# First weights in two half transfers, rounded by the vector engine alone, and the sink row's transfer on another queue

## The chip, the cores and the metric

The kernel runs on one core of one Trainium2 chip. The metric is the time of one execution on the device in microseconds (us); lower is better. A core has five engines that work at the same time, each through a queue of instructions of its own, in order: TensorE (PE in the profile, with its weight loads as PEld), VectorE (DVE), ScalarE (ACT), GpSimd (POOL) and SyncE (SP), which here does nothing but issue transfers between memory and the on-chip buffers. ACT and POOL issue transfers too. An instruction that has to wait for a semaphore holds up everything behind it in its engine's queue.

## The reference

A two-layer encoder on 256 tokens of 1024 values, in float32. Layer 0 mixes tokens with a gated short convolution, layer 1 with windowed attention (16 heads, 4 key and value heads, a window of 128 tokens, a relative bias and one "sink" logit per head). After each mixer stands the same kind of expert layer, called PEER. Cut to what matters:

```python
for i in range(2):
    x = x + (conv_mixer if i == 0 else attention)(rmsnorm(x, g[i]))
    x = x + peer(rmsnorm(x, ffn_g[i]), ...)
return rmsnorm(x, final_norm_g)

# conv mixer:  gate_b, gate_c, h = split(x @ w_in, 3);  (gate_b * conv3(gate_c * h)) @ w_out
# attention:   softmax over [scores + bias, sink] (the sink column is dropped afterwards)
# peer:        per token and head, top 16 of 16384 experts by two sub-key products, then
#              sum over the picked e of  softmax(gate)[e] * gelu(x . u[e]) * v[e]
```

## The kernel before, in words

**Split numbers.** TensorE multiplies in a rounded float32 format. To keep precision, every weight tile (128 x 1024) and every activation is held as two parts: the rounded value `hi` and the remainder `lo = raw - hi`. A product is three products: hi by hi, lo by hi, hi by lo. So each weight tile goes through three steps: SP's queue issues its transfer into `raw` (four buffers), an engine rounds it into `hi` (three buffers), and DVE subtracts to get `lo` (two buffers). The function `split_tile` does this. In the usual form ACT rounds (line 197) and DVE makes the remainder of the whole tile (line 198). A buffer comes free only when its last reader is done, so a late `lo` on DVE also delays the transfers that reuse `raw`.

**The beginning.** The convolution mixer starts with `turned_x` (its `else` branch, lines 490 to 512). PE first multiplies zeros (`keep_warm`), transposes the input `x` into `xn`, and multiplies zeros twice more. ACT scales the eight transposed pieces k = 0 to 7 into `xn[:, k, :T]` (line 502), except k = 1, which DVE does (line 499). Then the first weight tile is prepared by a form of `split_tile` of its own: one transfer of 512 KB, and three casts, of columns 0 to 255 and 256 to 511 on DVE and 512 to 1023 on POOL (line 190); DVE then makes the remainder in two halves (line 194) and the remainders of `xn` (line 508). The next two weight tiles come in the usual form, but rounded by ACT in halves. `first_three` (line 273) writes out the order in which PE takes these three tiles: for the first one k = 0 to 5 of `hi`, k = 0 to 3 of `lo`, k = 6 and 7 of `hi`, then k = 4 to 7 of `lo`; after it the `hi` of the other two, and the rest. One k is 128 columns of the weight tile, so k = 0 to 3 is its first half.

**The expert layer.** `peer` runs over 128 rows of u (128 experts each) in its first half of the work, and over 128 rows of v in its second (the loop over j in steps of 2 at line 1353). The gates with which rows are weighted are put into tables in device memory by indirect transfers that add single values, issued by POOL (line 666). Part of them, the "far additions", go in 22 steps of four transfers; `far_pump` issues one step at a time: four during the last 16 rows of the first half of the work, then one for every two rows of v from j = 0 on. Later rows load their gates back from these tables (line 1277).

While the second half of layer 0's `peer` runs, `meanwhile` prepares the attention: from j = 64 on, every fourth j calls `prepare_attention(part)` with part 0, 1, 2 and so on. Part 0 takes the memory that the first 64 rows of layer 0 no longer need and loads the sink row into it, broadcast to 128 partitions (line 735); parts 0 to 7 load the bias (line 737); part 8 (j = 96) negates the sink row on DVE (line 1390).

**What sets the order.** The program is written as one stream. The framework draws up each engine's queue before the run: instructions go in the order of the code, but one whose inputs its plan holds to be ready may go ahead of earlier ones when its engine is free in that plan. Where the code says `with tc.issue_after(ins)`, what is traced inside on the engine of `ins` stays behind `ins`; instructions on other engines are not bound by it. `meanwhile` is called inside such a block, behind ACT's copy (line 1347) of the rows in hand. `bg.behind` is the last instruction of this kind on DVE. Semaphores for data are set by the framework.

Of the kernel before, what the change touches and what calls it, by code (L numbers as in the profile page):

```python
# [17 lines left out]
P = 128  # L18
T = 256
D = 1024  # L20
NT = T // P
KC = D // P
HEADS = 16
# [53 lines left out]
def trunk_kernel(  # L77
# [20 lines left out]
    nc = tc.nc  # L98
    V, S, G, PE = nc.vector, nc.scalar, nc.gpsimd, nc.tensor
# [11 lines left out]
    def matmul(*a, **k):  # L111
        newest[:] = [PE.matmul(*a, **k).ins]  # L112
        return newest[0]

    def transpose(*a):
        newest[:] = [PE.transpose(*a).ins]  # L116
        return newest[0]

    def in_turn():

        return tc.issue_after(newest[0])
# [53 lines left out]

    roomy = []

    def split_tile(src, spare=False, pieces=1, engines=()):
        raw = strm.tile([P, D], F32, tag="raw", name="raw", bufs=4)
        hi = strm.tile([P, D], F32R, tag="hi", name="hi", bufs=3)  # L180
        if roomy:
            roomy[0] = not roomy[0]
            spare = roomy[0]
        lo = strm.tile([P, D], F32R, tag="oh2" if spare else "lo", name="lo", bufs=2)
        nc.sync.dma_start(raw, src)
        halves = slice(0, D // 2), slice(D // 2, D)
        if engines:
            at = 0
            for n, engine in engines:
                engine.tensor_copy(hi[:, at : at + n], raw[:, at : at + n])  # L190
                at += n
            for c in halves:
                with tc.issue_after(bg.behind):
                    bg.behind = V.tensor_tensor(lo[:, c], raw[:, c], hi[:, c].bitcast(F32), ALU.subtract).ins
            return hi, lo
        for c in halves if pieces > 1 else (slice(0, D),):
            bg.rounded = S.copy(hi[:, c], raw[:, c]).ins  # L197
        bg.behind = V.tensor_tensor(lo, raw, hi.bitcast(F32), ALU.subtract).ins  # L198
        return hi, lo
# [22 lines left out]
    def take(n=2):  # L222

        prefetch(n)
        return ahead.popleft()

    def prefetch(n, *how):
        while order and len(ahead) < n:
            with ExitStack() as held:
                for ins in evicted:  # L230
                    held.enter_context(tc.issue_after(ins))
                ahead.append(split_tile(order.popleft(), *how))
# [40 lines left out]
    def first_three(b, act):  # L273

        w = [[a.rearrange("p (k c) -> p k c", k=KC) for a in take(3 - i)] for i in range(3)]
        turns = [(0, 0, k, 0) for k in range(6)] + [(0, 1, k, 0) for k in range(4)]
        turns += [(0, 0, k, 0) for k in (6, 7)] + [(0, 1, k, 0) for k in range(4, KC)]
        later = (1, 0, 0), (2, 0, 0), (0, 0, 1), (1, 0, 1), (2, 0, 1), (1, 1, 0), (2, 1, 0)
        turns += [(i, low, k, n) for i, low, n in later for k in range(KC)]
        for at, (i, low, k, n) in enumerate(turns):  # L280
            others = [turn[0] == i for turn in turns]
            with in_turn():
                matmul(
                    b[i], w[i][low][:, k], act[:, k, T * n : T * n + T],
                    start=not any(others[:at]), stop=not any(others[at + 1 :]),
                )
            if at == 5 * KC - 1:
                prefetch(1, True)
            if at == 8 * KC - 1:
                prefetch(2)  # L290
        chain[:] = newest
# [70 lines left out]
    def add_to_x(acc, t, h):  # L362
        c = slice(512 * h, 512 * h + 512)
        return V.tensor_tensor(xs[:, t, c], acc[t][h], xs[:, t, c], ALU.add).ins
# [26 lines left out]
    def turned_x(n, xn, last=None, opens=None):  # L391
# [30 lines left out]
        def turn_by_halves(i):  # L422

            t, h = parts[i]
            if i == 0:
                banks.extend(bank("g", "ptr").rearrange("p (k c) -> p k c", k=2) for _ in range(2))
            if h:
                own = [bank("acc", "ptr").rearrange("p (k c) -> p k c", k=4) for _ in range(1 + 2 * t)]
                banks.append([own[min(j, 2 * t)][:, j] for j in range(4)])
            for j in range(4):  # L430
                k = 4 * h + j
                to = banks[-1][j] if h else banks[j // 2][:, j % 2, P * t : P * t + P]
                transpose(to, xs[:, t, P * k : P * k + P], ident)
# [7 lines left out]
        def high_of(h, t=0):  # L441
            for j in range(4):
                k, c, b = parted(h, t, j)
                evicted[:] = [S.activation(xn[:, k, c], b, AF.Copy, scale=gain[:, n, k : k + 1]).ins]

        def low_of(h, t=0, j0=0, j1=4):
            for j in range(j0, j1):
                k, c, b = parted(h, t, j)
                V.scalar_tensor_tensor(
                    xn[:, k, T + c.start : T + c.stop], b, gain[:, n, k : k + 1], xn[:, k, c].bitcast(F32),  # L450
                    op0=ALU.mult, op1=ALU.subtract,
                )

        if last:
            acc, one = last
            parts = [(t, h) for h in range(2) for t in range(NT)]
            for i in range(2):
                one(*parts[i])
                add_to_x(acc, *parts[i])
            prefetch(1, True)  # L460
            turn_by_halves(0)
            one(*parts[2])
            added = add_to_x(acc, *parts[2])
            turn_by_halves(1)
            high_of(0)
            with tc.issue_after(added):
                low_of(0, 0, 0, 3)

            def third():
                with in_turn():  # L470
                    turn_by_halves(2)
                high_of(1, 0)

            one(*parts[3], between=third)
            added = add_to_x(acc, *parts[3])
            with tc.issue_after(added):
                low_of(0, 0, 3, 4)
                low_of(1, 0)
            product = opened(opens, ahead.popleft(), xn)
            next(product)  # L480
            with in_turn():
                turn_by_halves(3)
            high_of(1, 1)
            low_of(1, 1)
            for _ in product:
                pass
            prefetch(1)
            evicted[:] = [bg.rounded]
        else:
            own = [bank("acc" if i > 1 else "g", "ptr").rearrange("p (k c) -> p k c", k=2) for i in range(6)]  # L490
            banks.extend([own[k][:, 0] if k < 4 else own[2 + k // 2][:, k % 2] for k in range(KC)])
            for t in range(NT):
                for k in range(KC):
                    turned = transpose(banks[k][:, P * t : P * t + P], xs[:, t, P * k : P * k + P], ident)
            with tc.issue_after(turned):
                keep_warm(WARM[1])
            for k in range(KC):
                if k == 1:
                    bg.behind = V.tensor_scalar(xn[:, k, :T], banks[k], gain[:, n, k : k + 1], None, op0=ALU.mult).ins
                else:  # L500
                    evicted[:] = [
                        S.activation(xn[:, k, :T], banks[k], AF.Copy, scale=gain[:, n, k : k + 1]).ins  # L502
                    ]
            with tc.issue_after(bg.behind):
                prefetch(1, False, 1, ((T, V), (T, V), (D // 2, G)))
            for k in range(KC):
                with tc.issue_after(bg.behind):
                    bg.behind = V.scalar_tensor_tensor(
                        xn[:, k, T:], banks[k], gain[:, n, k : k + 1], xn[:, k, :T].bitcast(F32),
                        op0=ALU.mult, op1=ALU.subtract,  # L510
                    ).ins
            prefetch(3, False, 2)
# [218 lines left out]
    def load_bias(sc, part):  # L731

        if part == 0:
            sc.held = sc(HEADS, 384), sc(HEADS)
            nc.scalar.dma_start(sc.held[1], bass.AP(tensor=sink.tensor, offset=sink.offset, ap=[[0, P], [1, HEADS]]))
        h = 2 * part
        nc.scalar.dma_start(
            sc.held[0][:, h : h + 2],
            bass.AP(
                tensor=bias_dram.tensor,  # L740
                offset=bias_dram.offset + h * 511,
                ap=[[1, P], [511, 2], [1, 384]],
            ),
        )
# [635 lines left out]
    sc = Scratch("HA", "mix0")  # L1380
# [169 lines left out]
```

## Time and profile before

| | |
|---|---|
| median of 3 runs | 1732.43 us (1732.32 to 1732.75) |
| the profiled execution: time, span | 1732.49 us, 1730.7 us |
| PE busy | 1722.7 us |
| DVE, ACT, POOL busy | 1384.9, 944.3, 970.3 us |
| transfers | 390.93 MB, mean 226 GB/s |

The span is the profiled part of the execution, from the first to the last instruction that the profiler records. A row of the timeline has the start, the length, the engine, the line of the code, the operation, the tile written and the tile read, their shapes, and how many instructions were merged into the row; in brackets stands how long the engine was idle before it and what ended that. "ACTq" or "POOLq" is the issue of a transfer by that engine. `pv`, `ph` and `pconv` are accumulators of PE; `raw`, `hi` and `lo` are the weight tiles; `mix` is scratch memory, which the sink row and the bias share. A row of the stretches has the window, its length, the busy time of PE, PEld, DVE, ACT and POOL, each with its count, the granted clock, the share of the transfer engines and GB/s. A row of the groups has the busy time and the mean in ns behind the bar, then the idle time before the group and what ended it. A row of transfer issues ends with the median time from issue to landing.

### The profile page before, as it was taken

Reading aid. Unit: us, or ns where it says so; the run is one execution under the profiler, and the core shown is the slowest. Engines: PE = TensorE matmul, PEld = TensorE weight load, DVE = VectorE, ACT = ScalarE, POOL = GpSimd, SP = SyncE. Lnnn points to the kernel's source line nnn. Section 1 sums busy time; section 2 is a strip of 40 time slices with the busy share of each in tenths; the row PEclk is TensorE's granted clock in tenths of the full one; section 3 lists DMA queues with packets and bytes.
Section 4 is the critical chain, followed back from the end, with each engine's and each line's share of the span. In section 5 each row is a group of like instructions: output and inputs, shape, how many; then the busy total and the mean of one; then the engine's idle time right before and its main releaser. Section 6 shows DMA issues by size and latency. Waiting matters only on the chain.

```text
span 1730.7 us, 28360 instructions
## 1 busy us (share of the span) xinstructions
PE 1722.7 (100%) x9795; PEld 1484.5 (86%) x9795; DVE 1384.9 (80%) x2986; ACT 944.3 (55%) x1255; POOL 970.3 (56%) x595
## 2 busy tenths in 40 slices
PE   9999999999999999999999999999999999999998
PEld 8989888888898888888898898888888888888887
DVE  8879999888777677777686899998887867777776
ACT  5456665565555444444476656655655544444444
POOL 2003888878888888000000048888788888881000
PEclk9999999999999999999999999999999999999999
DMA  7786998777779999998665779977766889998884
GB/s 259 253 284 206 281 280 195 172 185 183 180 181 237 228 233 240 297 288 256 227 208 174 258 209 281 262 195 171 188 177 170 213 231 230 235 244 267 258 260 139
DMA packets 292256, 390.93 MB, mean 226 GB/s; under 512 B 120192, under 2 KB 209824, under 8 KB 291856
## 3 DMA queue, kind: packets, MB, share of 16 engines
q1 hardware_dynamic: 86544, 314.35, 54.1%
q0 software_dynamic: 80144, 22.83, 14.8%
q10 hardware_dynamic: 125424, 51.96, 11.5%
q8 instruction: 76, 1.25, 0.3%
q14 instruction: 68, 0.56, 0.1%
HBM read 353.08 MB, written 35.95 MB: 225 GB/s over the span
## 4 chain that ended last, share of the span: by engine, by line
PE 99%; ACT 0%; DVE 0%; issue 0%; ACTq 0%
PE ph L112 41%; PE pv L112 41%; PE pq L112 7%; PE pconv L112 3%; PE pgate L112 1%; PE psc L112 1%; PE pwo L112 1%; PE pout L112 1%; PE pg L112 1%; PE ppt L116 0%; PE po L112 0%; PE ptr L116 0%; PE pk L112 0%; PE pwarm L112 0%; ACT xn L502 0%; PE pend L112 0%
## 5 line engine op out<-in xcount | busy, mean ns | idle before, releaser
L198 DVE TENSOR_TENSOR lo<-raw,hi 128x1024 fp32r<-128x1024 f32 x595 | 721.0, 1220 | 197.2 <-ACT hi L197 134.0
L197 ACT CAST hi<-raw 128x1024 fp32r<-128x1024 f32 (+1 forms) x597 | 623.5, 1047 | 448.5 <-PE pv L112 172.5
L666 POOL DMA_INDIRECT table<-route x256 | 445.7, 1741 | 129.8 <-issue 72.8
L112 PE MATMUL pv<-hi,xn 128*128 128x512 f32 (+1 forms) x2048 | 507.8, 389 | 0.0
L112 PE MATMUL ph<-xn,hi 128*128 128x512 f32 (+1 forms) x2112 | 492.2, 384 | 0.0
L112 PEld LDWEIGHTS pv<-hi,xn 128*128 128x128 f32 x2048 | 384.2, 188 | 79.6
L112 PEld LDWEIGHTS ph<-xn,hi 128*128 128x128 f32 x2112 | 381.5, 188 | 70.5
L666 POOL DMA_INDIRECT far_table<-yb x192 | 359.3, 1871 | 58.5 <-issue 54.2
L112 PE MATMUL pv<-lo,xn 128*128 128x512 f32 x1024 | 276.9, 390 | 0.0
L112 PE MATMUL ph<-xn,lo 128*128 128x256 f32 x2048 | 270.1, 283 | 0.0
L112 PEld LDWEIGHTS ph<-xn,lo 128*128 128x128 f32 x2048 | 262.5, 191 | 8.4
L112 PEld LDWEIGHTS pv<-lo,xn 128*128 128x128 f32 x1024 | 191.5, 188 | 39.3 <-DVE lo L198 0.3
L1277 POOL DMA_DIRECT2D far_gates<-far_table x44 | 23.8, 541 | 248.8 <-DMA gates<-table 78.3
L654 POOL DMA_DIRECT2D table<-blank x16 | 18.7, 1170 | 208.9 <-DVE lo L198 170.2
L666 POOL DMA_INDIRECT set_table<-yb x64 | 113.9, 1780 | 26.6 <-issue 26.6
L1347 ACT CAST xn<-hm 128x512 fp32r<-128x512 f32 x64 | 39.6, 622 | 74.2 <-PE pv L112 70.8
L1348 DVE TENSOR_TENSOR xn<-hm,xn 128x512 fp32r<-128x512 f32 x64 | 44.0, 690 | 36.8 <-ACT xn L1347 36.7
L324 ACT COPY hm<-ph 128x512 f32<-128x512 f32 x62 | 36.4, 586 | 56.4 <-PE ph L112 56.4
L1347 ACT CAST xn<-route 128x512 fp32r<-128x512 f32 x64 | 39.8, 622 | 49.5 <-PE pv L112 48.6
L1348 DVE TENSOR_TENSOR xn<-route,xn 128x512 fp32r<-128x512 f32 x64 | 44.1, 689 | 26.6 <-ACT xn L1347 26.6
L112 PE MATMUL pq<-xr,hi 128*128 128x512 f32 (+1 forms) x288 | 64.9, 371 | 0.0
L1323 ACT ACTIVATE hm<-hm 128x512 f32<-128x512 f32 x62 | 39.1, 631 | 44.5 <-DVE hm L325 44.5
(229 smaller groups left out, 1511.7 us busy)
## 6 DMA issues: line engine op xcount, KB each, us to landing
raw<-in_u SPq DMA_DIRECT2D x256, 512.0 KB
raw<-in_v SPq DMA_DIRECT2D x256, 512.0 KB
table<-blank POOLq DMA_DIRECT2D x16, 1024.0 KB, 8.3
raw<-in_w_q SPq DMA_DIRECT2D x32, 512.0 KB
gates<-table ACTq DMA_DIRECT2D x128, 128.0 KB
raw<-in_w_in SPq DMA_DIRECT2D x24, 512.0 KB
far_table<-blank ACTq DMA_DIRECT2D x10, 1024.0 KB
far_gates<-far_table ACTq DMA_DIRECT2D x156, 64.0 KB
```

What stands on the lines that cost most here:

```text
L112: newest[:] = [PE.matmul(*a, **k).ins]
L197: bg.rounded = S.copy(hi[:, c], raw[:, c]).ins
L198: bg.behind = V.tensor_tensor(lo, raw, hi.bitcast(F32), ALU.subtract).ins
L324: S.copy(dst, b[:, :, T:])
L654: ins = queue.dma_start(dst, blank[:, None, :].to_broadcast([P, dst.shape[1], P])).ins
L666: nc.gpsimd.indirect_dma_start(to, bass.IndirectOffsetOnAxis(ap=places[:, c : c + 1], axis=0), gates[:, c : c + 1], None, compute_op=ALU.a ...
L1277: ins = (nc.gpsimd if i == 2 else nc.scalar).dma_start(f[:, i], part.rearrange("p (a e t) -> p a e t", a=2, e=2)).ins
L1323: S.activation(hm[:, j : j + 2], hm[:, j : j + 2], AF.Gelu)
L1347: copied[:] = [S.copy(a[:, 0], src).ins]
L1348: return V.tensor_tensor(a[:, 1], src, a[:, 0].bitcast(F32), ALU.subtract).ins
```

## The change

Three things are changed.

1. `split_tile` has a form `halved` in place of the form with three casts. The first weight tile is fetched by two transfers of 512 columns each. DVE rounds the first half and makes its remainder, then does the same with the second. POOL no longer takes part.
2. `first_three` takes the first tile half by half: k = 0 to 3 of `hi`, k = 0 to 3 of `lo`, k = 4 to 7 of `hi`, k = 4 to 7 of `lo`. What follows is unchanged.
3. The transfer of the sink row in `load_bias` is issued by POOL in place of ACT. The call stays at its place in the code.

```diff
-    def split_tile(src, spare=False, pieces=1, engines=()):
+    def split_tile(src, spare=False, pieces=1, halved=False):
 ...
-        nc.sync.dma_start(raw, src)
         halves = slice(0, D // 2), slice(D // 2, D)
-        if engines:
-            at = 0
-            for n, engine in engines:
-                engine.tensor_copy(hi[:, at : at + n], raw[:, at : at + n])
-                at += n
+        if halved:
+            for c in halves:
+                nc.sync.dma_start(raw[:, c], src[:, c])
             for c in halves:
                 with tc.issue_after(bg.behind):
+                    V.tensor_copy(hi[:, c], raw[:, c])
                     bg.behind = V.tensor_tensor(lo[:, c], raw[:, c], hi[:, c].bitcast(F32), ALU.subtract).ins
             return hi, lo
+        nc.sync.dma_start(raw, src)
 ...
-        turns = [(0, 0, k, 0) for k in range(6)] + [(0, 1, k, 0) for k in range(4)]
-        turns += [(0, 0, k, 0) for k in (6, 7)] + [(0, 1, k, 0) for k in range(4, KC)]
+        turns = [(0, low, k, 0) for k0 in (0, KC // 2) for low in range(2) for k in range(k0, k0 + KC // 2)]
 ...
-                prefetch(1, False, 1, ((T, V), (T, V), (D // 2, G)))
+                prefetch(1, False, 1, True)
 ...
-            nc.scalar.dma_start(sc.held[1], bass.AP(tensor=sink.tensor, offset=sink.offset, ap=[[0, P], [1, HEADS]]))
+            nc.gpsimd.dma_start(sc.held[1], bass.AP(tensor=sink.tensor, offset=sink.offset, ap=[[0, P], [1, HEADS]]))
```

## The prediction

> **What bounds the kernel now.** I read the page first (busy shares, then the chain that ended last), then the timeline of the first 13 us engine by engine, and then the timeline around the place to which the second part of the change belongs, 675 to 725 us.
>
> ```profile
> span 1730.7 us, 28360 instructions
> PE 1722.7 (100%) x9795; PEld 1484.5 (86%) x9795; DVE 1384.9 (80%) x2986; ACT 944.3 (55%) x1255; POOL 970.3 (56%) x595
> ```
> ```profile
> PE 99%; ACT 0%; DVE 0%; issue 0%; ACTq 0%
> ```
>
> TensorE is busy in 1722.7 of 1730.7 us and is 99% of the chain, so the time is PE's start plus a stream of matmuls that nothing interrupts. A microsecond saved before the stream starts is kept to the end. A microsecond for which PE has to wait anywhere is lost. The profiled execution took 1732.49 us (1.8 us around its span), 0.06 above the median of 1732.43.
>
> **The change at the start.** PE and the engines that feed it:
>
> ```profile
> 1.08 4.02 PE L112 MATMUL pwarm<-blank 128*128 128x512 bf16 x9 [1.08 <-DVE blank L171]
> ...
> 7.12 0.59 PE L112 MATMUL pwarm<-blank 128*128 128x512 bf16 x2
> 7.34 0.38 PE L112 MATMUL pwarm<-blank 128*128 128x512 bf16 x1
> 7.89 1.32 PE L112 MATMUL pconv<-xn,hi 128*128 128x256 f32 x6 [0.17 <-ACT xn L502]
> ...
> 10.43 1.12 PE L112 MATMUL pconv<-xn,hi 128*128 128x256 f32 x8
> ```
> ```profile
> 6.56 2.67 ACT L502 ACTIVATE xn<-ptr,gain 128x256 fp32r<-128x256 f32 x7 [3.88 <-PE ptr L116]
> 9.07 2.22 ACT L197 CAST hi<-raw 128x512 fp32r<-128x512 f32 x4
> 6.67 0.48 DVE L499 TENSOR_SCALAR xn<-ptr,gain 128x256 fp32r<-128x256 f32 x1 [1.42 <-PE ptr L116]
> 7.45 0.29 DVE L190 CAST hi<-raw 128x256 fp32r<-128x256 f32 x1 [0.30 <-DMA raw<-in_w_in]
> 7.66 0.70 DVE L190 CAST hi<-raw 128x256 fp32r<-128x256 f32 x1
> 7.56 0.65 POOL L190 CAST hi<-raw 128x512 fp32r<-128x512 f32 x1 [4.07 <-DMA raw<-in_w_in]
> 8.39 0.69 DVE L194 TENSOR_TENSOR lo<-raw,hi 128x512 fp32r<-128x512 f32 x1
> 9.00 0.68 DVE L194 TENSOR_TENSOR lo<-raw,hi 128x512 fp32r<-128x512 f32 x1
> 9.60 3.22 DVE L508 SCALAR_TENSOR_TENSOR xn<-ptr,gain,xn 128x256 fp32r<-128x256 f32 x8
> 40.97 0.42 DVE L715 CAST mix<-mix 97x511 bf16<-97x511 f32 x1
> ```
> ```profile
> 6.00:7.00 1.00, 1.00 (x9) 0.81 (x8) 0.33 (x1) 0.44 (x2) 0.00 (x0) 1.00 1.03 422
> ```
>
> The first tile's 16 matmuls run from 7.89 to 10.43. Eight matmuls in a row take 1.12 us of which the last takes about 0.28, so they start 0.12 apart; 16 would need 1.92 us, and 0.6 is stalls. DVE stands idle 0.30 us for the weights, and its second cast (0.70 beside POOL's cast, where the one before took 0.29) delays the remainders.
>
> New chain on DVE. Landing: 512 KB at 422 GB/s is 1.24 us, half of it 0.62, so the first half can be used at about 7.45 - 0.62 = 6.83, before DVE ends L499 at 7.15. Cast of 512 columns: the trace has none alone on DVE to this type; the nearest row is 0.42 (L715, 511 columns), the upper bound 0.70 (half the columns beside a busy POOL, which is now idle); I take 0.42. First half: cast 7.15 to 7.57, remainder to 8.26 (0.69). The next operation starts 0.61 after a remainder (8.39 to 9.00): second cast 8.18 to 8.60, remainder to 9.29. L508 then starts at 9.21 in place of 9.60.
>
> New chain on PE. Its first matmul came 0.15 after the cast ended (7.74 to 7.89): now 7.72, four matmuls to 8.27. First remainders from 8.32, with 0.1 to restart, to 8.90. High parts of k 4 to 7 need ACT's last L502 (6.56 + 2.67 = 9.23): the last runs at about 9.38. Remainders of the second half follow to 9.98. So the second tile starts at 9.98, not 10.43: **0.45 us gained**. Bounds: not before about 9.93, by L502 (gain 0.5); and with no half landing before 7.45 and casts of 0.70, the last remainder ends at 7.45 + 0.70 + 0.61 + 0.70 + 0.69 = 10.15, and PE comes at 10.76 (loss 0.33). What is next would still be in time: w1 is rounded from 9.07 in halves 0.55 apart, w2 by 11.29, its second half needed at 9.98 + 0.96 + 0.48 = 11.42; L508 moves forward by 0.39 with PE. POOL loses a cast that nobody else waited behind; the additional transfer on SP's queue is hidden by the transfers already waiting in front of it.
>
> **The change at j = 64.** The sink row's transfer (L735) goes from ACT's queue to POOL's. On ACT it saves one issue, which is worth nothing, as ACT is 55% busy. What counts is who waits for it and what stands ahead of it on POOL.
>
> ```profile
> 678.89 0.34 ACTq L735 DMA_DIRECT2D mix<-in_sink  x1
> ```
> ```profile
> 677.13 1.21 DVE L198 TENSOR_TENSOR lo<-raw,hi 128x1024 fp32r<-128x1024 f32 x1
> 679.19 0.69 DVE L1348 TENSOR_TENSOR xn<-route,xn 128x512 fp32r<-128x512 f32 x1 [0.85 <-ACT xn L1347]
> ...
> 680.20 1.22 DVE L198 TENSOR_TENSOR lo<-raw,hi 128x1024 fp32r<-128x1024 f32 x1
> ...
> 684.54 0.33 DVE L1390 TENSOR_SCALAR mix<-mix 128x16 f32<-128x16 f32 x1 [2.59 <-DMA mix<-in_sink]
> ...
> 685.13 1.22 DVE L198 TENSOR_TENSOR lo<-raw,hi 128x1024 fp32r<-128x1024 f32 x1
> ```
> ```profile
> 684.00 1.07 PE L112 MATMUL pv<-lo,xn 128*128 128x512 f32 x4
> ...
> 686.72 1.07 PE L112 MATMUL pv<-lo,xn 128*128 128x512 f32 x4
> ```
> ```profile
> 692.05 1.96 POOL L666 DMA_INDIRECT far_table<-yb  x1 [0.30 <-issue]
> 723.03 0.63 POOL L1277 DMA_DIRECT2D far_gates<-far_table  x1 [29.02 <-DMA gates<-set_table]
> ```
> ```profile
> L666 POOL DMA_INDIRECT far_table<-yb x26 | 46.4, 1786 | 7.9 <-issue 7.9
> ```
> ```profile
> far_table<-yb POOLq DMA_INDIRECT x17, 5.0
> ```
>
> L1390, which negates the sink, stands in the code at part 8 (j = 96), not pinned by an issue_after. It ran at 684.54, 5.65 us after its transfer's issue: the framework, which draws up every queue before the run, pulls it forward to just behind the transfer. DVE works its queue in order, so everything behind L1390 waits too, here 2.59 us. PE does not notice, but only just: the remainders ready at 681.42 (680.20 + 1.22) are used at 684.00, 2.58 us later; those behind the stall are ready at 686.35 and used at 686.72, with 0.37 to spare.
>
> On POOL the last step of far additions (four indirect transfers each) stands in the code at j = 34: 22 steps, four in the half before, one for each two rows after. The trace shows POOL far behind the code: when ACT is at j = 64 (678.89), POOL is still in these steps, 26 of them from 640 to 694 with nothing but 0.30 us of issue between them, the last ending at 692.05 + 1.96 = 694.01. A transfer that the code puts behind them goes out at 694.3. On that queue a transfer lands 5.0 us after its issue; at the start, POOL's plain transfers took 3.5:
>
> ```profile
> mix<-in_buckets POOLq DMA_DIRECT2D x3, 63.9 KB, 3.5
> ```
>
> I take 4.3, between the two: the sink is there at 698.6 (697.8 to 699.3). No wait or order in the code ties L1390's place to POOL's lateness.
>
> Where L1390 stands in DVE's queue decides the rest. On POOL the transfer isn't bound to come after ACT's copy at j = 64 (L1347, whose remainder L1348 is), only after the last use of the scratch's memory, two rows earlier. So the plan can send it, and take L1390, earlier than now. (a) Behind the L198 of 677.13, in the gap of 0.85 before L1348: I take this, as it is the first idle gap of DVE there. After the landing come L1390 to the next operation (684.54 to 685.13, 0.59), L1348 to the next L198 (679.19 to 680.20, 1.01) and L198 (1.22): remainders at 698.6 + 2.82 = 701.4, which PE wanted at 684.00: **PE waits 17.5 us**. Two other places:
>
> ```profile
> 676.08 0.65 DVE L1213 TENSOR_REDUCE oh<-pg 128x160 f32<-128x480 f32 x1
> ```
> ```profile
> 681.28 1.07 PE L112 MATMUL pv<-lo,xn 128*128 128x512 f32 x4
> ```
>
> (b) Ahead of L1213: 0.59 + 1.05 (676.08 to 677.13) + 1.21, and PE wanted those at 681.28: 20.2. (c) Where it is now: 0.59 + 1.22, wanted at 686.72: 13.7. The landing adds -0.8 to +0.7 to each.
>
> After the wait PE may start slowly. At the start nine pwarm matmuls take 4.02 us, about 0.43 from one to the next; of the two at 7.12 the second (7.34) follows after 0.22. So PE ran at half speed for its first 3.9 us (nine times 0.43) and lost half of them, 1.9 us. After 17 idle us I count **1.9** once more (bounds 0 and 1.9: no stall of this length is in the trace). On this the Trainium skill, in "TensorE: Matmul & The Clock Gate", Part 1: The HAM clock gate, says that an idle stretch of about 3.4 us halves PE's clock and that about 3.4 us of work bring it back; by that alone the term would be an estimated 1.7 us. The first row above agrees in kind, with 3.9 us. Another rule would speak for a harmless move: in "DMA: Bandwidth & Descriptors", Specifications, the skill gives a first byte after about 1 us from GpSimd's queue and 0.6 from ScalarE's, an estimated 0.4 us more, and the sum by it would be 1732.0. It speaks of an empty queue; POOL's row shows a full one.
>
> Sum: 1732.49 - 0.45 + 17.5 + 1.9 = **1751.4 us**. Lowest of the slow case: (c) with the early landing, no slow clock and a lost start gain, 1732.5 + 13.7 - 0.8 = 1745; highest, (b) with the late landing: 1732.5 - 0.45 + 20.2 + 0.7 + 1.9 = 1754.9.
>
> **The rivals.** *L1390 keeps its place* (c), 1732.49 - 0.45 + 13.7 + 1.9 = 1747.6: it holds if the plan sends the transfer no earlier than ACT does now. Against it: nothing on POOL's queue says so.
>
> *Not slower: the sink is in time.* It decides at 684.9: if the row lands by then (now 684.54, and 0.37 to spare), PE loses nothing and only the start counts, 1732.0. This needs POOL to send the transfer ahead of its indirect transfers, or the plan to put L1390 where the code has it, 32 rows (some 87 us at 2.72 a row) later. For it: both orders are the framework's, not the code's. Against it: POOL's order follows the code as far as the trace shows it (L1277 of later rows comes after the steps), and the same operation was pulled forward in this trace.
>
> *The start doesn't gain:* the second remainders come later than now, up to 0.33 lost; alone that gives 1732.8, on top of the main case 1752.2. For it: DVE now does all the casts that POOL shared; against it: beside POOL, DVE's own cast grew from 0.29 to 0.70.
>
> **How the numbers follow.** About 0.2% (3.5 us) is what a measurement of this kernel can tell from no change. Chances: (a) 0.50, (b) 0.15, (c) 0.20, some other stall of over 3.5 us from the sink 0.02, in time 0.11, faster by over 0.2% 0.02 (nothing in PE's 8 idle us offers it). The start's gain or loss shifts any of them by under 0.5 and decides no sign. So slower 0.87, same 0.11, faster 0.02. The range 1743.5 to 1756 takes in (a), (b) and (c) with their bounds; in time and faster lie outside it.
>
> **What would show it.** In the profile after: w1's first matmul near 9.98 and L508 at 9.2 (start). L735 on POOL after an L666, at 694 or so; L1390 with an idle time of 14 to 22 us released by the sink's transfer; one PE gap of 13 to 20 us ending near 701, with matmuls 0.4 apart behind it. It is wrong if L735 runs on POOL before 684, if L1390 has no wait, or if PE's busy time stays within 10 us of its span.

## The result, and the profile after

The changed kernel takes 1749.44 us (median of 5 runs, 1747.78 to 1749.60) against 1732.43 before: a ratio of 1.0096, with a 95% interval of 1.0085 to 1.0108. It is slower by 17 us. The profiled execution took 1747.78 us, 15.29 more than the one shown of before.

The page of the changed kernel (busy shares, PE's row of the 40 slices, the chain by engine and by line). Since the change moved the line numbers, L198, L666, L735, L1348 and L1390 of before are L197, L664, L733, L1346 and L1388 here:

```profile
span 1746.0 us, 28363 instructions
PE 1725.2 (99%) x9795; PEld 1486.5 (85%) x9795; DVE 1383.6 (79%) x2986; ACT 943.4 (54%) x1255; POOL 956.3 (55%) x595
...
PE   9999999999999996999999999999999999999998
...
PE 92%; POOL 4%; issue 2%; DMA 2%; DVE 0%; ACT 0%; POOLq 0%; ACTq 0%
PE ph L112 41%; PE pv L112 33%; PE pq L112 6%; POOL far_table L664 4%; PE pconv L112 3%; DMA far_table<-yb 2%; PE pgate L112 1%; PE psc L112 1%; PE pwo L112 1%; PE pout L112 1%; PE pg L112 1%; PE ppt L116 0%; PE po L112 0%; PE ptr L116 0%; PE pk L112 0%
```

PE's row of the slices in the kernel before:

```profile
PE   9999999999999999999999999999999999999998
```

PE has as many matmuls as before, but the span is 15.3 us longer. One slice, the 16th (655 to 698 us), has fallen from 9 to 6, and a new engine stands in the chain: POOL with its far additions, where PE alone had 99%. The chain leaves PE in that slice and runs back along POOL's queue.

The timeline of the changed kernel there, first DVE, then PE, then POOL:

```profile
675.74 0.65 DVE L1211 TENSOR_REDUCE oh<-pg 128x160 f32<-128x480 f32 x1
692.53 0.17 DVE L1388 TENSOR_SCALAR mix<-mix 128x16 f32<-128x16 f32 x1 [16.14 <-DMA mix<-in_sink]
692.61 0.42 DVE L1190 TENSOR_TENSOR route<-oh,route 128x160 f32<-128x160 f32 x1
692.95 1.22 DVE L197 TENSOR_TENSOR lo<-raw,hi 128x1024 fp32r<-128x1024 f32 x1
```
```profile
679.13 1.98 PE L112 MATMUL pv<-hi,xn 128*128 128x512 f32 x8
694.22 2.08 PE L112 MATMUL pv<-lo,xn 128*128 128x512 f32 x4 [13.11 <-DVE lo L197]
696.09 3.34 PE L112 MATMUL pv<-hi,xn 128*128 128x512 f32 x8
699.27 1.08 PE L112 MATMUL pv<-lo,xn 128*128 128x512 f32 x4
```
```profile
688.09 1.54 POOL L664 DMA_INDIRECT far_table<-yb  x1 [0.30 <-issue]
689.07 1.20 POOL L733 DMA_DIRECT2D mix<-in_sink  x1
```

Read from the bottom: POOL sends the sink row at 689.07, directly behind its last indirect transfer. DVE had asked for it at 676.39 (675.74 + 0.65) and stands until 692.53. Behind L1388 in its queue wait one operation and the remainders of a weight tile, which PE needs. PE has work until 681.1, then stands for 13.11 us. Then four matmuls take 2.08 us and eight 3.34, where 1.07 and 1.98 are usual: from 694.22 to 699.27 PE does in 5.05 us what takes 2.72, another 2.33 us. The sum closes when the wait, too, is counted from start to start, because the modelled end of a matmul runs into the next one. PE before, at the same place:

```profile
679.47 1.98 PE L112 MATMUL pv<-hi,xn 128*128 128x512 f32 x8
681.28 1.07 PE L112 MATMUL pv<-lo,xn 128*128 128x512 f32 x4
```

There the next matmuls start 1.81 us after the eight; here they start 15.09 us after them (679.13 to 694.22), which is 13.28 us lost. With the 2.33 us, and less the 0.34 us by which PE was ahead at this place (679.13 against 679.47), that is 15.27 of the 15.3 us.

The start of the changed kernel, PE and DVE:

```profile
7.22 0.59 PE L112 MATMUL pwarm<-blank 128*128 128x512 bf16 x2
7.73 0.71 PE L112 MATMUL pconv<-xn,hi 128*128 128x256 f32 x4
8.36 0.74 PE L112 MATMUL pconv<-xn,lo 128*128 128x256 f32 x4
...
10.07 1.12 PE L112 MATMUL pconv<-xn,hi 128*128 128x256 f32 x8
```
```profile
7.17 0.42 DVE L191 CAST hi<-raw 128x512 fp32r<-128x512 f32 x1
7.62 0.69 DVE L192 TENSOR_TENSOR lo<-raw,hi 128x512 fp32r<-128x512 f32 x1
8.22 0.42 DVE L191 CAST hi<-raw 128x512 fp32r<-128x512 f32 x1
8.68 0.69 DVE L192 TENSOR_TENSOR lo<-raw,hi 128x512 fp32r<-128x512 f32 x1
```

The second tile (10.07) comes 0.36 us earlier than before (10.43), although PE's second warming pair, which follows the transposes of `x`, began 0.10 later (7.22 against 7.12). Counted from that pair the way to the second tile has shrunk from 3.31 to 2.85 us: 0.46. All profiles of this case agree on it: 3.30 to 3.35 us in the three with the old start (before, sink_only, sink_again), 2.84 to 2.92 in the eight with the whole new one. DVE's first cast no longer waits for its transfer, and a cast of 512 columns costs 0.42.

### The profile page after: what moved, and what is told of

Same layout as the page of the kernel before. It is cut to its first block, busy times and chain, and to the rows that moved or that the text cites. A ratio compares the mean times of both kernels' runs of the same rounds, so it can differ in the third digit from the quotient of the medians.

```text
span 1746.0 us, 28363 instructions
## 1 busy us (share of the span) xinstructions
PE 1725.2 (99%) x9795; PEld 1486.5 (85%) x9795; DVE 1383.6 (79%) x2986; ACT 943.4 (54%) x1255; POOL 956.3 (55%) x595
## 4 chain that ended last, share of the span: by engine, by line
PE 92%; POOL 4%; issue 2%; DMA 2%; DVE 0%; ACT 0%; POOLq 0%; ACTq 0%
PE ph L112 41%; PE pv L112 33%; PE pq L112 6%; POOL far_table L664 4%; PE pconv L112 3%; DMA far_table<-yb 2%; PE pgate L112 1%; PE psc L112 1%; PE pwo L112 1%; PE pout L112 1%; PE pg L112 1%; PE ppt L116 0%; PE po L112 0%; PE ptr L116 0%; PE pk L112 0%
## 5 line engine op out<-in xcount | busy, mean ns | idle before, releaser
L197 DVE TENSOR_TENSOR lo<-raw,hi 128x1024 fp32r<-128x1024 f32 x595 | 721.3, 1221 | 200.6 <-ACT hi L196 138.5
L664 POOL DMA_INDIRECT table<-route x256 | 442.6, 1729 | 129.9 <-issue 73.1
L664 POOL DMA_INDIRECT far_table<-yb x192 | 349.9, 1822 | 58.5 <-issue 53.9
L664 POOL DMA_INDIRECT set_table<-yb x64 | 112.6, 1759 | 27.2 <-issue 27.2
L1346 DVE TENSOR_TENSOR xn<-hm,xn 128x512 fp32r<-128x512 f32 x64 | 44.0, 690 | 37.0 <-ACT xn L1345 37.0
L1346 DVE TENSOR_TENSOR xn<-route,xn 128x512 fp32r<-128x512 f32 x64 | 44.0, 688 | 25.8 <-ACT xn L1345 25.8
```

The lines of the kernel that those rows point to most:

```text
L664: nc.gpsimd.indirect_dma_start(to, bass.IndirectOffsetOnAxis(ap=places[:, c : c + 1], axis=0), gates[:, c : c + 1], None, compute_op=ALU.a ...
L1346: return V.tensor_tensor(a[:, 1], src, a[:, 0].bitcast(F32), ALU.subtract).ins
```

## The experiments

Theory A is that of the prediction: the loss is the sink row's place in POOL's late queue, and the way from there over L1388 and DVE to PE. Rival B: the new start disturbs the order of the queues later on. Rival C: a transfer by POOL is slow in itself, whatever stands ahead of it. The profiles above already speak against C: DVE got the row 3.46 us after POOL's issue (689.07 to 692.53), and 5.65 us after ACT's in the kernel before (678.89 to 684.54).

### The start alone

```diff
--- changed kernel
+++ begin_only
-            nc.gpsimd.dma_start(sc.held[1], bass.AP(tensor=sink.tensor, ...))
+            nc.scalar.dma_start(sc.held[1], bass.AP(tensor=sink.tensor, ...))
```

> The changed kernel with the sink row's transfer back on ACT's queue: the start as changed, nothing else. Theory A (POOL's late queue holds the sink row, L1388 holds DVE, PE waits): all of the loss is gone and the start's gain is left, 1732.43 - 0.36 = 1732.1 us (second tile's first matmul near 10.07 against 10.43 before). Rival B (the new start disturbs the later order of the queues): still about 1749. Rival C (a transfer by POOL is slow in itself): 1732.1 too.

Measured: 1732.34 us (11 runs) against 1732.39 for the kernel before on the same chip, ratio 0.9999 (0.9990 to 1.0008). The loss is gone, which is against B. The start's gain doesn't show in the time. In the profile it is there, 2.85 us from the second warming pair to the second tile:

```profile
7.01 0.59 PE L112 MATMUL pwarm<-blank 128*128 128x512 bf16 x2
...
9.86 1.12 PE L112 MATMUL pconv<-xn,hi 128*128 128x256 f32 x8
```

DVE's wait at L1388 is again a hidden one:

```profile
683.34 0.17 DVE L1388 TENSOR_SCALAR mix<-mix 128x16 f32<-128x16 f32 x1 [1.95 <-DMA mix<-in_sink]
```

### The sink's transfer alone

```diff
--- kernel before
+++ sink_only, sink_again
-            nc.scalar.dma_start(sc.held[1], bass.AP(tensor=sink.tensor, ...))
+            nc.gpsimd.dma_start(sc.held[1], bass.AP(tensor=sink.tensor, ...))
```

> The kernel before with the sink row's transfer on POOL and nothing else changed. Theory A: the whole loss, without the start's gain: 1749.4 + 0.36 = 1749.8 us, one PE gap of 12 to 16 us before 695. Rival B (the new start is the cause): 1732.4. Rival C (a transfer by POOL is slow in itself): 1749.8 too.

Measured: 1759.18 us, ratio 1.0157 (1.0140 to 1.0174). The old start with the moved transfer is slow, so B falls for good; but it is 9.4 us slower than expected. POOL was later here: it sent the row at 700.13, not 689.07:

```profile
700.13 1.21 POOL L735 DMA_DIRECT2D mix<-in_sink  x1
```

So the changed kernel ran again beside this one, on another chip.

> The changed kernel once more, beside the kernel with the sink's transfer alone moved and two with steps left out, on one chip. sink_only took 1759.2 where 1749.8 was expected, because POOL's last indirect transfer began at 699.2 and not at 688.1. If this comes from the chip or the run and not from the kernels' start, this kernel lands within 1 us of sink_again, 0.4 below it; if the old start (POOL's cast, one transfer) makes POOL later, this kernel is some 10 us below sink_again.

> The kernel before with only the sink row's transfer on POOL, once more. By the chip: after_again + 0.4 us. By the kernel's start: some 1759 us wherever it runs, after_again 10 below.

Measured on that chip: the changed kernel 1758.22 (1757.12 to 1760.63), the transfer alone 1758.13 (1756.83 to 1759.51), before 1732.33. The two are alike, and the changed kernel is itself 8.8 us above its first measurement: the difference was not the kernels'. That neither lies 10 us below the other also answers the expectation. The timeline of the changed kernel in this run (DVE, POOL, PE):

```profile
703.63 0.18 DVE L1388 TENSOR_SCALAR mix<-mix 128x16 f32<-128x16 f32 x1 [27.30 <-DMA mix<-in_sink]
...
700.07 1.20 POOL L733 DMA_DIRECT2D mix<-in_sink  x1
...
705.31 2.08 PE L112 MATMUL pv<-lo,xn 128*128 128x512 f32 x4 [24.27 <-DVE lo L197]
```

Most of the time that POOL lost is seen in its groups from 480 to 510 us, first in the first run of the changed kernel, then in this one:

```profile
L664 POOL DMA_INDIRECT far_table<-yb x11 | 18.7, 1697 | 3.4 <-issue 3.4
L664 POOL DMA_INDIRECT set_table<-yb x5 | 8.8, 1751 | 1.5 <-issue 1.5
```
```profile
L664 POOL DMA_INDIRECT far_table<-yb x6 | 15.5, 2578 | 1.8 <-issue 1.8
L664 POOL DMA_INDIRECT set_table<-yb x6 | 11.9, 1980 | 1.8 <-issue 1.8
```

It issued 16 transfers there in one run and 12 in the other, because single issues took up to 3.6 us. Up to 462 us the two queues run 0.15 us apart. From 466 us on, pairs of issues that take 2.56 and 1.56 us in the first run take 3.50 and 3.57 in the other, three times over, and by 515 us it is 11 us behind. Why they did isn't settled, nor whether the chip or the run decides it.

### Less of POOL's queue ahead of the row

```diff
--- changed kernel
+++ steps_out1, steps_out2, steps_out2_again, steps_out4 (n = 1, 2, 2, 4)
         far_steps = deque([(h, i) for i in range(SETS - 1) for h in range(0 if i else 2, PH)])
+        if layer == 0:
+            for _ in range(n):
+                far_steps.pop()
```

> The changed kernel with the last one of layer 0's 22 steps of far additions left out (four indirect transfers of POOL, so four gates per token and one table are missing from the output). Theory A: POOL reaches the sink row 4 x 1.85 = 7.4 us earlier, and PE's wait falls by as much: 13.1 - 7.4 = 5.7 us in the profile, with some slow matmuls behind it: 1741 to 1742 us. Rival C: the landing does not depend on what stands ahead in POOL's queue: 1749.4.

> The changed kernel with the last two of layer 0's steps of far additions left out (eight indirect transfers). Theory A: the sink row is sent 14.8 us earlier, near 674.5, and lands near 678, some 1.5 us after DVE asks for it; PE has 2.6 us to spare, so no PE gap is left: 1732.1 us. Rival C: 1749.4.

> The changed kernel without the last two steps of far additions of layer 0 (eight indirect transfers of POOL; gates are missing from the output), once more. Theory A on one chip: 8 x 1.85 = 14.8 us less of POOL's queue ahead of the sink row, so after_again - 14.8 us, but not below 1732.1. If nothing in POOL's queue counts: the same as after_again.

> The changed kernel without the last four steps of far additions of layer 0 (16 indirect transfers, 29.6 us of POOL's queue). Theory A: on a chip with the early or the late POOL the sink row is now in time: no PE gap of over 1 us, 1732.0 us. If the software transfer is slow in itself, or the plan's place of L1388 alone costs time: as after_again.

The absolute times expected of the first two (1741 to 1742 and 1732.1) were wrong, as they started from the early POOL of the first run. The differences on one chip hold. The estimate of 1.85 us a transfer is the usual 1.54 us of an issue and the 0.30 us to the next; on the first chip the kernel with all its steps is sink_only, which has the old start (on the second chip the two starts came out 0.1 us apart):

| chip | steps left out | time, us | change, us | change by 1.85 us a transfer |
|---|---|---|---|---|
| first | 0 (sink_only) | 1759.18 | | |
| first | 1 | 1751.06 | -8.1 | -7.4 |
| first | 2 | 1743.88 | -15.3 | -14.8 |
| second | 0 (after_again) | 1758.22 | | |
| second | 2 | 1743.59 | -14.6 | -14.8 |
| second | 4 | 1732.65 | -25.6 | -29.6, but not below 1732 |

Without four steps the kernel is where it was before (1.0002, 0.9992 to 1.0012), with the same transfer by POOL, and with the negation at the same place in DVE's queue (here L1391, directly behind L1211). So neither the transfer by POOL in itself (C) nor the place alone is what costs, but what stands ahead of the row. The rows of DVE, POOL and PE, two steps left out (first chip):

```profile
689.08 0.17 DVE L1391 TENSOR_SCALAR mix<-mix 128x16 f32<-128x16 f32 x1 [12.53 <-DMA mix<-in_sink]
...
685.53 1.20 POOL L733 DMA_DIRECT2D mix<-in_sink  x1
...
690.76 2.08 PE L112 MATMUL pv<-lo,xn 128*128 128x512 f32 x4 [9.51 <-DVE lo L197]
```

and DVE and POOL with four left out:

```profile
677.14 0.18 DVE L1391 TENSOR_SCALAR mix<-mix 128x16 f32<-128x16 f32 x1 [0.84 <-DMA mix<-in_sink]
...
673.97 0.62 POOL L733 DMA_DIRECT2D mix<-in_sink  x1 [2.05 <-DVE xn L1349]
```

In each of the seven stalled profiles PE starts again 5.1 to 5.4 us after POOL's issue (689.07 to 694.22, 700.07 to 705.31 and 685.53 to 690.76 in the rows shown). With four left out POOL is idle for 2.05 us and waits for DVE's L1349 (L1346 of the changed kernel), behind which the memory is free; the row is there 3.2 us after the issue, DVE waits 0.84, PE not at all.

### The negation pinned where the code has it

```diff
--- changed kernel
+++ after_pinned
         elif part == PH:
-            V.tensor_scalar(held[0].held[1], held[0].held[1], -1.0, None, op0=ALU.mult)
+            with tc.issue_after(bg.behind):
+                V.tensor_scalar(held[0].held[1], held[0].held[1], -1.0, None, op0=ALU.mult)
```

> The changed kernel with the sink row's transfer on POOL as it is, and the operation that negates the row (L1388 of the changed kernel) held behind DVE's last remainder at part 8, where the code has it. Theory A: nobody asks for the row until some 80 us after POOL sends it, so no wait is left: 1732.1 us. Rival B: about 1749. Rival C: 1732.1, since no transfer takes 80 us.

Measured: 1731.98 us (11 runs, 1731.72 to 1732.25) against 1732.39, ratio 0.9997 (0.9988 to 1.0006). POOL sends the row as late as ever, and nobody minds (POOL's row, then DVE's):

```profile
694.88 1.20 POOL L733 DMA_DIRECT2D mix<-in_sink  x1
```
```profile
778.61 0.17 DVE L1389 TENSOR_SCALAR mix<-mix 128x16 f32<-128x16 f32 x1
```

The row arrives some 80 us before its reader. This is the repaired form of the change: some 17 us below the first measurement of the changed kernel, and not to be told from the kernel before.

### The parts of the start

Both start from begin_only:

```diff
--- begin_only
+++ one_transfer
-            for c in halves:
-                nc.sync.dma_start(raw[:, c], src[:, c])
+            nc.sync.dma_start(raw, src)
--- begin_only
+++ old_order
-        turns = [(0, low, k, 0) for k0 in (0, KC // 2) for low in range(2) for k in range(k0, k0 + KC // 2)]
+        turns = [(0, 0, k, 0) for k in range(6)] + [(0, 1, k, 0) for k in range(4)]
+        turns += [(0, 0, k, 0) for k in (6, 7)] + [(0, 1, k, 0) for k in range(4, KC)]
```

> The kernel of begin_only with the first tile in one transfer of 512 KB; casts on DVE alone and PE by halves stay. If the half transfer is what brings the gain, DVE's first cast waits until about 7.45 in place of 7.17, the chain on DVE ends 0.28 later and the second tile's first matmul comes near 10.3: 1732.35 us. If the casts without POOL and the order on PE bring it, 10.07 and 1732.1.

> The kernel of begin_only with the old order of PE for the first tile (high parts k 0 to 5 first); two transfers and DVE alone stay. High parts 4 and 5 then wait for the second cast (ends 8.64 in the changed kernel) ahead of the first remainders, but the end is set by the second remainder (9.37) and four matmuls: second tile near 10.1 to 10.2, so 1732.1 to 1732.25 us. If the order on PE is what brings the gain: 10.4 and 1732.45.

Measured: 1732.25 and 1732.10 us, ratios 0.9998 (0.9989 to 1.0008) and 0.9998 (0.9989 to 1.0007): the times tell neither apart from the kernel before or from begin_only. The timelines do. PE with one transfer, with DVE's first cast below; then PE in the old order:

```profile
6.95 0.59 PE L112 MATMUL pwarm<-blank 128*128 128x512 bf16 x2
7.86 0.71 PE L112 MATMUL pconv<-xn,hi 128*128 128x256 f32 x4 [0.32 <-DVE hi L190]
...
10.14 1.12 PE L112 MATMUL pconv<-xn,hi 128*128 128x256 f32 x8
...
7.29 0.43 DVE L190 CAST hi<-raw 128x512 fp32r<-128x512 f32 x1 [0.31 <-DMA raw<-in_w_in]
```
```profile
7.63 0.59 PE L112 MATMUL pwarm<-blank 128*128 128x512 bf16 x2
...
10.71 0.52 PE L112 MATMUL pconv<-xn,hi 128*128 128x256 f32 x3
```

From the second warming pair to the second tile it takes 3.19 us with one transfer and 3.08 in the old order, against 2.85 with all three and 3.31 before. Each of these two is needed: without the half transfers 0.34 of the 0.46 us is gone, without the order by halves 0.23. Counting from the pair is fair to the transfer, too: in the four profiles with one transfer DVE's first cast starts 0.31 to 0.36 us after the pair, wherever the pair stands. The casts on DVE alone were not taken back by themselves, so their share is not shown. The absolute places in the expectations (10.3, 10.1 to 10.2) missed because the pair itself, which waits for the transposes of `x`, began between 6.63 and 7.63 in these runs. That spread is twice the gain, and it is why a true 0.46 us can't be read from a time.

## Why the prediction was right, and where its terms were off

**The bound.** PE's stream has no slack: PE's wait and slow work, less its lead, are found again in the span (15.27 of 15.3 us).

**The start.** Predicted 0.45 us gained, measured 0.46 from the warming pair to the second tile; in the time it can't be seen. The cast of 512 columns, taken at 0.42 from L715, took 0.42; the first half did not hold DVE up.

**The sink row.** The mechanism held at each step: the transfer stood behind the far additions, DVE's order put the negation far ahead of its place in the code, and PE waited for the remainders behind it. The terms of the sum were off, and partly cancelled.

- *When POOL sends the row.* Predicted 694.3, measured 689.07 in the profile shown and 700.07 on a later chip. The chain of POOL was taken from one execution. In the five profiles in which nothing waits for it and no step is left out, its last far addition begins anywhere from 691.79 (one_transfer) to 695.89 (begin_only), and the time doesn't show it; in the two of the changed kernel at 688.09 and 699.09. This was the largest error, of either sign: the predicted 1751.4 lies between 1749.4 and 1758.2, and the second measurement of the same kernel lies above the range. That the first came within 2 us of the forecast is in part luck.
- *Landing.* Predicted 4.3 us from issue to landing, measured 3.43 in the chain of waits of the changed kernel:

```profile
689.07 3.43 DMA mix<-in_sink
```

- *Where L1388 stands.* Place (a) was held the likeliest; it is nearly (b), one operation later: behind L1211 (which is L1213 of before) and not ahead of it, well before (a)'s gap. So the prediction's likeliest place was not the right one. What had to follow the landing was then only L1388, L1190 and L197: 692.53 to 694.22, 1.69 us where (a) counted 2.82 and (b) 2.85. The three small copies of L777 that stood behind L1390 went behind the remainders.
- *When PE wants the remainders.* Since L1388 stands earlier, it held back those of an earlier tile: PE wanted them at 680.94 (679.13 + 1.81) and not at 684.00. This alone makes the wait 3.1 us longer.

PE's wait, from start to start, came out as 13.28 us where the sum had 17.5 (its own terms give 17.4: 698.6 + 2.82 - 684.00). The first three terms took off 5.2, 0.9 and 1.1 us, the fourth put 3.1 on.

**The slow restart.** Predicted 1.9 us, measured 2.33: twelve matmuls in 5.05 us where 2.72 are usual. The granted clock was 0.53 in these 5.05 us, and 1.00 from 681.28 to 684.00 before. The Trainium skill, in "TensorE: Matmul & The Clock Gate", Part 1, gives half the clock after an idle stretch and some 3.4 us until it is back. The trace agrees with the half rate: four matmuls take 2.08 us there and 1.07 usually. The slow matmuls fill more than 4 of the 5.05 us, so 3.4 is too short for this stall; the same Part also puts the change at around 4 us of sustained work, give or take 0.5, and that fits better.

**The rivals.** "In time" was wrong for this kernel, but right about its condition: with four steps left out the row comes in time, and the kernel is as fast as before. That L1390 keeps its place (c) was wrong too. "The start doesn't gain" was wrong by the profiles; the times can't tell.

## What to carry to other kernels

A transfer moved to another engine's queue has to be judged by what stands ahead of it there when it is really issued, not by what the engine's busy share or the code's order suggests: POOL was 56% busy over the span, and full just there. Look at who waits for a transfer in its engine's order, and how much the bound engine has to spare behind that: the kernel before already had 2.59 us of DVE's wait hidden with 0.37 us to spare. Where a framework may pull an operation forward to its transfer, pin it to the place at which the code needs it; that alone made the move free.

## What was not expected of the hardware

- POOL's indirect transfers take less time while DVE stands still. The groups of POOL from 676 to 689 us, before and then changed:

```profile
L666 POOL DMA_INDIRECT far_table<-yb x7 | 13.6, 1944 | 2.1 <-issue 2.1
```
```profile
L664 POOL DMA_INDIRECT far_table<-yb x8 | 13.3, 1665 | 2.4 <-issue 2.4
```

Here an issue takes 1.54 us while DVE stands, and up to 2.6 beside a working DVE. The last seven far additions begin within 11.08 us in the changed kernel (677.01 to 688.09), and within 11.99 us (before) to 14.44 us (begin_only) in the five profiles in which DVE works on. The Trainium skill ("SBUF — State Buffer", SBUF: two separate sides) says that some operations of DVE keep GpSimd from the port through which it writes a transfer's descriptors until they end. These rows agree with that, but PE, ACT and most transfers stand still there as well, and no experiment here took single operations of DVE away, so the cause is argued and not shown.

- The same kernel took 1749.4 us on one chip and 1758.2 on another, while the kernel before took 1732.4 and 1732.3 there. A time that hangs on POOL's queue inherits its spread, so an effect of 7 us is only seen within one chip, beside the kernel that it is compared with.
